# Rotary embedding on one core: the order of three loads on the SP queue

## The chip, the core and the metric

The kernel runs on one core of a Trainium2 chip. The metric is device time in microseconds for one execution, inputs and outputs in device memory (HBM). A core has compute engines that run side by side: TensorE (PE, unused here), VectorE (DVE), ScalarE (ACT) and GpSimd (POOL), and SyncE (SP), which here only issues transfers. Transfers are carried by 16 DMA engines, which all queues share. This kernel uses two queues: SP's, "hardware_dynamic" in the profile, and GpSimd's, "software_dynamic".

## The reference

```python
# x (8, 2048, 16, 64) float32; cos, sin (2048, 32) float32
x_pairs = x.reshape(batch, seq_len, num_heads, head_dim // 2, 2)
x1 = x_pairs[..., 0]
x2 = x_pairs[..., 1]
cos = cos[None, :, None, :].copy()
sin = sin[None, :, None, :].copy()
out1 = x1 * cos - x2 * sin
out2 = x1 * sin + x2 * cos
out = np.stack([out1, out2], axis=-1).reshape(batch, seq_len, num_heads, head_dim)
```

Neighbouring elements of a row form pairs, and each pair is turned by an angle that depends on the position in the sequence and the place in the head. x and the output are 67.1 MB each.

## The kernel before

The work is cut by batch: eight tiles, each a whole batch. Of the 2048 positions a partition holds 16 (`K`), so a batch is a tile of 128 partitions x 16 x 1024 elements: 64 KB a partition in HBM, 32 KB as bfloat16 in SBUF. A load (`load`, line 56) converts from float32 to bfloat16 on the way in, a store (`store`, line 59) converts back on the way out, and both are issued from the GpSimd queue. The pool `xpool` has five tiles (`NX`); batches 5, 6 and 7 take over the tiles of batches 0, 1 and 2, and so their loads wait until those batches are stored.

`rotate` (lines 61 to 80) does the arithmetic in three VectorE instructions: x times a signed sine table into a work tile `qt` (L74), x times a cosine table in place (L75), and the sum of x and `qt` with each pair of `qt` swapped (L80).

The two tables are made once: `sin_sb` and `cos_sb` are loaded from HBM as float32 (256 KB each, 2 KB a partition) and cast by VectorE into `s_tab` (the sine and its negative in turns, L93 and L94) and `c_tab` (each cosine twice, L95).

Batch 0 is split. Its first two positions of each partition (`HEAD`), one megabyte, go by the SP queue as float32 into `head` (line 84), and ScalarE casts them into the tile of batch 0 (L91). The rest of batch 0 comes by the GpSimd queue (`load(0, HEAD)`), followed by batches 1 to 4 whole. So there are two rotations for batch 0, a small one and a large one, and one for every other batch. `head` and `qt` share one buffer (the tag "work", one buffer), so the first rotation also waits until ScalarE has read `head`.

The order is written out by hand (`manual_schedule`): each engine runs its instructions in the order of the program text. On SP these are the megabyte of x (L84), the cosine table (L85), the sine table (L86) and, at the very end, the last store (L119). On GpSimd: five loads; the store of batch 0; a small copy called `mark` (L106), which reads the last element of batch 4 and so holds up all that stands behind it until the fifth load has landed; the store of batch 1; then the load of batch 5, the store of batch 2, the load of batch 6, the store of batch 3, the load of batch 7, and the stores of batches 4 to 7, the last without its final four positions (`TAIL`). Those are cast back by ScalarE (L118) and stored by SP (L119); a one-element copy before them (L117) waits for the store of batch 6.

Of the kernel before, what the change touches and what calls it, by code (L numbers as in the profile page):

```python
# [2 lines left out]

# [4 lines left out]


@with_exitstack  # L10
def kernel(
    ctx: ExitStack,
    tc: tile.TileContext,
    x: bass.AP,
    cos: bass.AP,
    sin: bass.AP,
    out: bass.AP,
):
    nc = tc.nc
    fp32 = mybir.dt.float32  # L20
    bf16 = mybir.dt.bfloat16
    mult = mybir.AluOpType.mult
    add = mybir.AluOpType.add

    B, S, H, D = x.shape
    P = 128
    K = S // P
    KP = 16
    D2 = D // 2
    HD = H * D  # L30
    NX = 5
    HEAD = 2
    TAIL = 4


    x_t = x.rearrange("b (p k) h d -> b p k (h d)", p=P, k=K)
    out_t = out.rearrange("b (p k) h d -> b p k (h d)", p=P, k=K)
    cos_t = cos.rearrange("(p k) c -> p (k c)", p=P, k=K)
    sin_t = sin.rearrange("(p k) c -> p (k c)", p=P, k=K)

    consts = ctx.enter_context(tc.tile_pool(name="consts", bufs=1))
    xpool = ctx.enter_context(tc.tile_pool(name="xpool", bufs=NX))
    stage = ctx.enter_context(tc.tile_pool(name="stage", bufs=1))

    cos_sb = consts.tile([P, K * D2], fp32)
    sin_sb = consts.tile([P, K * D2], fp32)
    c_tab = consts.tile([P, K, D], bf16)
    s_tab = consts.tile([P, K, D], bf16)

    mark = consts.tile([1, 1], bf16)  # L50
    tiles = {}

    def load(b, k0=0):
        if b not in tiles:
            tiles[b] = xpool.tile([P, K, HD], bf16, name="xt")
        nc.gpsimd.dma_start(out=tiles[b][:, k0:], in_=x_t[b, :, k0:])  # L56

    def store(b, k1=K):
        nc.gpsimd.dma_start(out=out_t[b, :, :k1], in_=tiles[b][:, :k1])  # L59

    def rotate(b, k0, k1):
        nk = k1 - k0
        xp = tiles[b][:, k0:k1]
        qt = stage.tile([P, KP, HD], bf16, name="qt", tag="work")

        def rows(a):
            return a.rearrange("p k (h e) -> p k h e", h=H, e=D)

        def tab(a):
            return dataclasses.replace(  # L70
                a, offset=a.offset + k0 * D, ap=[a.ap[0], [D, nk], [0, H], [1, D]]
            )

        nc.vector.tensor_tensor(out=rows(qt[:, :nk]), in0=rows(xp), in1=tab(s_tab), op=mult)  # L74
        nc.vector.tensor_tensor(out=rows(xp), in0=rows(xp), in1=tab(c_tab), op=mult)  # L75
        q_swap = dataclasses.replace(
            qt, offset=qt.offset + 1, ap=[qt.ap[0], [2, nk * HD // 2], [-1, 2]]
        )
        x3 = xp.rearrange("p k (a j) -> p (k a) j", j=2)
        nc.vector.tensor_tensor(out=x3, in0=x3, in1=q_swap, op=add)  # L80

    with tc.manual_schedule():
        head = stage.tile([P, TAIL, HD], fp32, name="st", tag="work")
        nc.sync.dma_start(out=head[:, :HEAD], in_=x_t[0, :, :HEAD])  # L84
        nc.sync.dma_start(out=cos_sb, in_=cos_t)  # L85
        nc.sync.dma_start(out=sin_sb, in_=sin_t)  # L86
        load(0, HEAD)
        for b in range(1, NX):
            load(b)

        nc.scalar.copy(out=tiles[0][:, :HEAD], in_=head[:, :HEAD])  # L91
        s2 = s_tab.rearrange("p k (i j) -> p (k i) j", j=2)
        nc.vector.tensor_copy(out=s2[:, :, 0], in_=sin_sb)  # L93
        nc.vector.tensor_scalar_mul(s2[:, :, 1], sin_sb, -1.0)  # L94
        nc.vector.tensor_copy(  # L95
            out=c_tab.rearrange("p k (i j) -> p (k i) j", j=2),
            in_=cos_sb.to_broadcast([P, K * D2, 2]),
        )
        for b in range(B):
            if b == 0:  # L100
                rotate(b, 0, HEAD)
                rotate(b, HEAD, KP)
            else:
                rotate(b, 0, KP)
            if b == 1:
                nc.gpsimd.tensor_copy(out=mark, in_=tiles[NX - 1][:1, K - 1, :1])  # L106
            if b < B - 1:
                store(b)

            if b >= 1 and b - 1 + NX < B:  # L110
                load(b - 1 + NX)
        store(B - 1, K - TAIL)

        tail = stage.tile([P, TAIL, HD], fp32, name="st", tag="work")
        nc.scalar.copy(out=tiles[B - 2][:1, 0, :1], in_=tiles[B - 1][:1, K - 1, :1])  # L117
        nc.scalar.copy(out=tail, in_=tiles[B - 1][:, K - TAIL :])  # L118
        nc.sync.dma_start(out=out_t[B - 1, :, K - TAIL :], in_=tail)  # L119


# [1 line left out]
_INS = ['x', 'cos', 'sin']  # L123
_OUTS = [((8, 2048, 16, 64), 'float32')]


# [23 lines left out]
```

## Time and profile before

| what | us |
|---|---|
| time, median of 3 runs (317.43 to 317.56) | 317.45 |
| span of the profiled execution | 315.5 |
| VectorE busy | 210.3 |
| ScalarE busy | 6.9 |
| GpSimd busy | 11.7 |
| megabyte of x: from issue to landing | 4.7 |
| cosine table: from issue to landing | 13.4 |
| sine table: from issue to landing | 31.7 |
| first load (rest of batch 0): from issue to landing | 22.3 |

The span runs from the first to the last instruction of the profiled execution, and the time shown for a run is a little longer than it. Lines of the page's first part give each engine's busy time, share of the span and instructions; the row "DMA" gives the mean busy share of the 16 DMA engines in 40 equal slices, in tenths. For a queue the page gives packets, megabytes (as written by the transfer) and the time of its packets as a share of 16 engines' span. In the order of time an entry has its start and its duration in microseconds, the engine, the line of the kernel, the operation, destination and source, and in brackets how long the engine was idle before it and what ended that. An entry of SPq or POOL with DMA_DIRECT2D is the issuing of a transfer, not the transfer. In the table of windows the columns are the window, its length, the busy time of VectorE, ScalarE and GpSimd (with instructions in brackets), the granted TensorE clock, the share of the 16 DMA engines and GB/s. All in all HBM was read for 67.63 MB and written for 67.11 MB.

### The profile page before, as it was taken

Reading aid. Unit: us, or ns where it says so; the run is one execution under the profiler, and the core shown is the slowest. Engines: PE = TensorE matmul, PEld = TensorE weight load, DVE = VectorE, ACT = ScalarE, POOL = GpSimd, SP = SyncE. Lnnn points to the kernel's source line nnn. Section 1 sums busy time; section 2 is a strip of 40 time slices with the busy share of each in tenths; the row PEclk is TensorE's granted clock in tenths of the full one; section 3 lists DMA queues with packets and bytes.
Section 4 is the critical chain, followed back from the end, with each engine's and each line's share of the span. In section 5 each row is a group of like instructions: output and inputs, shape, how many; then the busy total and the mean of one; then the engine's idle time right before and its main releaser. Section 6 shows DMA issues by size and latency. Waiting matters only on the chain.

```text
span 315.5 us, 125 instructions
## 1 busy us (share of the span) xinstructions
DVE 210.3 (67%) x30; ACT 6.9 (2%) x4; POOL 11.7 (4%) x21
## 2 busy tenths in 40 slices
DVE  0000799999999999999999993899509994000000
ACT  4000000000000000000000000000000000000400
POOL 3000000000000301010000100000000000000000
DMA  9899999999999999999999999999999999999997
GB/s 279 184 261 206 199 220 245 199 199 253 212 199 266 399 449 482 399 332 245 220 399 399 399 199 199 399 532 266 199 241 490 399 399 490 440 399 399 432 432 332
DMA packets 2880, 101.71 MB, mean 322 GB/s; under 512 B 320, under 2 KB 320, under 8 KB 576
## 3 DMA queue, kind: packets, MB, share of 16 engines
q0 software_dynamic: 2304, 98.04, 97.1%
q1 hardware_dynamic: 576, 3.67, 3.0%
HBM read 67.63 MB, written 67.11 MB: 427 GB/s over the span
## 4 chain that ended last, share of the span: by engine, by line
another core or an unknown queue 91%; DMA 1%; ACTq 1%; ACT 1%; issue 0%
DMA st<-in_x_dram 1%; ACTq L145 1%; ACT xt L91 1%; ACT xt L117 0%; ACTq L117 0%
## 5 line engine op out<-in xcount | busy, mean ns | idle before, releaser
L74 DVE TENSOR_TENSOR qt<-xt,s_tab 128x16384 bf16<-128x16384 bf16 (+2 forms) x9 | 69.7, 7743 | 19.1 <-DMA xt<-in_x_dram 18.8
L75 DVE TENSOR_TENSOR xt<-xt,c_tab 128x16384 bf16<-128x16384 bf16 (+2 forms) x9 | 69.7, 7743 | 0.4
L80 DVE TENSOR_TENSOR xt<-xt,qt 128x16384 bf16<-128x16384 bf16 (+2 forms) x9 | 69.7, 7744 | 0.3
L93 DVE CAST s_tab<-sin_sb 128x512 bf16<-128x512 f32 x1 | 0.5, 453 | 33.4 <-DMA sin_sb<-in_sin_dram 33.4
L59 POOL DMA_DIRECT2D out_dram<-xt x8 | 4.3, 534 | 139.9 <-DVE xt L80 139.9
L56 POOL DMA_DIRECT2D xt<-in_x_dram x8 | 4.4, 560 | 72.8 <-DMA out_dram<-xt 72.0
L117 ACT COPY xt<-xt 1x1 bf16<-1x1 bf16 x1 | 0.2, 192 | 288.0 <-DMA out_dram<-xt 288.0
L106 POOL COPY mark<-xt 1x1 bf16<-1x1 bf16 x1 | 2.9, 2929 | 39.6 <-DMA xt<-in_x_dram 39.6
L118 ACT CAST st<-xt 128x4096 f32<-128x4096 bf16 x1 | 3.6, 3598 | 0.0
L91 ACT CAST xt<-st 128x2048 bf16<-128x2048 f32 x1 | 1.9, 1897 | 3.4 <-DMA st<-in_x_dram 3.4
L91 ACT ACT_TABLE_LOAD x1 | 1.3, 1283 | 0.7 <-PEq L134 0.7
L95 DVE CAST c_tab<-cos_sb 128x1024 bf16<-128x1024 f32 x1 | 0.7, 683 | 0.0
L94 DVE TENSOR_SCALAR s_tab<-sin_sb 128x512 bf16<-128x512 f32 x1 | 0.4, 444 | 0.0
L134 POOL MEMSET const-float32-0.0<- 128x1 f32 x1 | 0.1, 100 | 0.2 <-issue 0.2
L134 POOL MEMSET const-bfloat16-1.0<- 128x1 bf16 x1 | 0.1, 102 | 0.0
L134 POOL MEMSET const-float32-1.0<- 128x1 f32 x1 | 0.1, 100 | 0.0
L134 POOL MEMSET const-uint8-127<- 128x1 uint8 x1 | 0.1, 100 | 0.0
## 6 DMA issues: line engine op xcount, KB each, us to landing
xt<-in_x_dram POOLq DMA_DIRECT2D x7, 4096.0 KB, 57.6
out_dram<-xt POOLq DMA_DIRECT2D x1, 6144.0 KB, 47.8
xt<-in_x_dram POOLq DMA_DIRECT2D x1, 3584.0 KB, 22.3
out_dram<-st SPq DMA_DIRECT2D x1, 2048.0 KB, 15.5
st<-in_x_dram SPq DMA_DIRECT2D x1, 1024.0 KB, 4.7
cos_sb<-in_cos_dram SPq DMA_DIRECT2D x1, 256.0 KB, 13.4
sin_sb<-in_sin_dram SPq DMA_DIRECT2D x1, 256.0 KB, 31.7
out_dram<-xt POOLq DMA_DIRECT2D x7, 70.1
```

The lines of the kernel that those rows point to most:

```text
L56: nc.gpsimd.dma_start(out=tiles[b][:, k0:], in_=x_t[b, :, k0:])
L59: nc.gpsimd.dma_start(out=out_t[b, :, :k1], in_=tiles[b][:, :k1])
L74: nc.vector.tensor_tensor(out=rows(qt[:, :nk]), in0=rows(xp), in1=tab(s_tab), op=mult)
L75: nc.vector.tensor_tensor(out=rows(xp), in0=rows(xp), in1=tab(c_tab), op=mult)
L80: nc.vector.tensor_tensor(out=x3, in0=x3, in1=q_swap, op=add)
L91: nc.scalar.copy(out=tiles[0][:, :HEAD], in_=head[:, :HEAD])
L93: nc.vector.tensor_copy(out=s2[:, :, 0], in_=sin_sb)
L94: nc.vector.tensor_scalar_mul(s2[:, :, 1], sin_sb, -1.0)
L95: nc.vector.tensor_copy(out=c_tab.rearrange("p k (i j) -> p (k i) j", j=2), in_=cos_sb.to_broadcast([P, K * D2, 2]),)
L106: nc.gpsimd.tensor_copy(out=mark, in_=tiles[NX - 1][:1, K - 1, :1])
L118: nc.scalar.copy(out=tail, in_=tiles[B - 1][:, K - TAIL :])
L145: with _tile.TileContext(nc) as tc:
```

## The change

The three issues at the head of the SP queue change places: cosine table, sine table, megabyte of x. The same three transfers are issued from the same queue, and the other queues and engines keep their instructions and their order.

```diff
     with tc.manual_schedule():
         head = stage.tile([P, TAIL, HD], fp32, name="st", tag="work")
-        nc.sync.dma_start(out=head[:, :HEAD], in_=x_t[0, :, :HEAD])
         nc.sync.dma_start(out=cos_sb, in_=cos_t)
         nc.sync.dma_start(out=sin_sb, in_=sin_t)
+        nc.sync.dma_start(out=head[:, :HEAD], in_=x_t[0, :, :HEAD])
         load(0, HEAD)
         for b in range(1, NX):
             load(b)
```

So lines 84, 85 and 86 are the cosine table, the sine table and the megabyte of x in the changed kernel; all other line numbers stay.

## The prediction

> **What bounds the kernel now.** I read the page first, for what is busy from end to end.
>
> ```profile
> span 315.5 us, 125 instructions
> DVE 210.3 (67%) x30; ACT 6.9 (2%) x4; POOL 11.7 (4%) x21
> DMA  9899999999999999999999999999999999999997
> q0 software_dynamic: 2304, 98.04, 97.1%
> q1 hardware_dynamic: 576, 3.67, 3.0%
> ```
>
> No compute engine is near full, but the packets of the two queues add up to 100.1% of sixteen engines' span. So the transfers are the bound, and nearly all are on q0, the GpSimd queue; q1 is SP's. Behind the 4% of GpSimd lies only the issuing. The counts also give the shape: 20 transfers (four on SP, sixteen on GpSimd) share 2880 packets, 144 each, nine on each of sixteen engines: eight rows of data (128 partitions over 16 engines) and one small closing packet (the page counts 320 under 512 B, which is 20 x 16).
>
> Second, the order of time, for what the moved transfers feed.
>
> ```profile
> 0.74 0.36 SPq L84 DMA_DIRECT2D st<-in_x_dram  x1
> 1.16 0.42 SPq L85 DMA_DIRECT2D cos_sb<-in_cos_dram  x1
> 1.24 2.80 POOL L56 DMA_DIRECT2D xt<-in_x_dram  x5 [0.80 <-PEq L145]
> 1.63 0.42 SPq L86 DMA_DIRECT2D sin_sb<-in_sin_dram  x1
> 5.45 1.90 ACT L91 CAST xt<-st 128x2048 bf16<-128x2048 f32 x1 [3.43 <-DMA st<-in_x_dram]
> 33.38 0.45 DVE L93 CAST s_tab<-sin_sb 128x512 bf16<-128x512 f32 x1 [33.38 <-DMA sin_sb<-in_sin_dram]
> 38.43 7.62 DVE L74 TENSOR_TENSOR qt<-xt,s_tab 128x14336 bf16<-128x14336 bf16 x1
> 61.93 0.54 POOL L59 DMA_DIRECT2D out_dram<-xt  x1 [57.89 <-DVE xt L80]
> 102.11 2.93 POOL L106 COPY mark<-xt 1x1 bf16<-1x1 bf16 x1 [39.64 <-DMA xt<-in_x_dram]
> 121.68 0.53 POOL L56 DMA_DIRECT2D xt<-in_x_dram  x1 [16.17 <-DMA out_dram<-xt]
> ```
>
> VectorE sits idle for 33.38 us until the sine table is there, although the first piece of x was there at 5.43. But the first store, issued at 61.93, lands only at 121.68, 19.6 us after the fifth load landed (102.11). By the rate of full transfers (8.39 MB in 19.3 us, below) 19.6 us is one store's own length: it had been waiting in the queue behind the loads. VectorE's lateness is hidden there.
>
> Third, short windows of the start, for what the transfer engines carry. The columns I use are the last two, DMA share and GB/s; a packet is counted whole in the window in which it begins, so that 6.00 to 7.00 shows nothing while long packets run.
>
> ```profile
> 1.00:2.00 1.00, 0.00 (x0) 1.00 (x1) 0.76 (x2) 1.00 0.39 66
> 2.00:3.00 1.00, 0.00 (x0) 0.02 (x1) 1.00 (x3) 1.00 0.74 254
> 3.00:4.00 1.00, 0.00 (x0) 0.00 (x0) 1.00 (x2) 1.00 1.00 418
> 4.00:5.00 1.00, 0.00 (x0) 0.00 (x0) 0.04 (x1) 1.00 0.93 375
> 5.00:6.00 1.00, 0.00 (x0) 0.55 (x1) 0.00 (x0) 1.00 2.50 602
> 6.00:7.00 1.00, 0.00 (x0) 1.00 (x1) 0.00 (x0) 1.00 0.00 0
> ```
>
> The loads begin with a burst a little after 5.0: one row of the first load on each of 16 engines is 3584 KiB / 8 = 459 KB, and the window has 602. The rest, 143 KB, and the windows before it are SP's: 66 + 254 + 418 + 375 + 143 = 1256 KB of the 1573 KB that its three transfers hold.
>
> **The change, part by part.** No instruction is added or removed; three issues on SP swap places, and the megabyte is passed by two transfers of 256 KB.
>
> *The tables.* They start at 0.74 and 1.16. The windows reach 524 KB (both tables) at 3.5 us; the megabyte, which had begun whole at about 4.8, landed at 5.43, so I add 0.6: landed at about 4.1 instead of 14.56 (1.16 + 13.4) and 33.3 (1.63 + 31.7). The three table casts (33.38 to 34.66, 1.28 us) run at 4.1 to 5.4.
>
> *The megabyte.* By the start of the loads 1256 KB have gone as before, of them now 1256 - 524 = 732 KB of its 1049: 5.6 rows of 8 on an engine. What is left takes turns with load rows. The trace shows the price of a turn: the sine table's nine packets landed 18.8 us after the cosine table, 2.09 us each. Two to four rows and the closing packet, three to five turns, end at 11.7 to 15.9; I take 14. The outer bounds are 6.2 (317 KB at the 418 GB/s of the full window, no turns) and 33.4 (27 packets of SP's, as before, if their number alone decides). None is later than the sine table now.
>
> *VectorE.* The ACT copy (1.90 us) ends at about 16, the small rotation (34.66 to 38.43, 3.8 us) at 20, and the next waits for the first load, which lands at 1.24 + 22.3 = 23.5 as before. So its big run starts at 23.5 instead of 38.43: 14.9 us gained on VectorE. What is late next is the loads: VectorE keeps its waits for the loads of batches 6 and 7, and gets a new one for batch 5.
>
> *The store queue, where the gain stops.* The first store is issued at 47 instead of 61.93, behind the same five loads, which end at 102. The next GpSimd step, the mark, waits for the fifth load at 102.11, not for VectorE; the sixth load waits for the first store to land. From there all issues have the same releasers: I cost the gain at nothing, and the cover is the loads' 102 us, 40 us longer than VectorE needed before.
>
> *The mark's phase.* The mark ended at 105.04 just as a vector multiply did (96.31 + 8.69 = 105.00). With VectorE shifted the multiply then running is that of batch 3 and ends at 107.6 (23.5 + 23.0 + 2 x 26.2 = 98.9, + 8.7). The second store is issued 2.6 us later, 13 us before the first has landed: no cost. If the queue did run dry here, up to 5 us.
>
> *The transfers themselves.* The bytes are the same. All of SP's packets cost 3.0% of 315.5 = 9.5 us on an engine; at 418 GB/s they would cost 8.8. So a better order can save at most 0.7 us. A worse one: the first window's 66 KB at a share of 0.39 are 169 GB/s, at which the tables would take 3.1 us instead of 1.25, +1.85 us. The nearest row is the one with full engines (418), as cold-start latency is paid once in either order: 0, perhaps -0.1.
>
> *The casts beside the first issues.* New is that VectorE works at 4.1 to 5.4 while the first loads get under way (GpSimd's five issues end at 4.04, the rows begin at 5.1). Lower bound 0. Upper: the rows start 1.1 us (5.1 - 4.04) after the casts, at 6.5 to 7.0, while SP's rows cover until 5.4 + 317/418 = 6.2: 0.3 to 0.8 us of idle engines. GpSimd's other issues beside busy VectorE took 0.53 to 0.54 us, no longer than beside an idle one, so I take 0.
>
> Here the Trainium skill speaks against the change ("SBUF — State Buffer", "SBUF: two separate sides"): transfers from the GpSimd queue need descriptors that GpSimd writes through a port which VectorE holds during some of its operations, and they starve until it is done. The mark agrees with a held port; no run here shows it for descriptors. By the rule the sum would be 0.3 to 0.8 us more, by the rows nothing.
>
> **Sum.** 315.5 + 0 - 0.1 = 315.4 us of span; the median, 317.45, lies 1.95 above the profiled span, and that part is not touched: 317.4 us.
>
> **Rivals.** *A: the earlier VectorE shortens the run.* For it: 33.4 us of idle time at the head. If VectorE were on the path, 317.45 - 14.9 = 302.6. Against it: its waits for batches 6 and 7.
>
> ```profile
> 198.72 8.69 DVE L74 TENSOR_TENSOR qt<-xt,s_tab 128x16384 bf16<-128x16384 bf16 x1 [6.40 <-DMA xt<-in_x_dram]
> 237.32 8.69 DVE L74 TENSOR_TENSOR qt<-xt,s_tab 128x16384 bf16<-128x16384 bf16 x1 [12.45 <-DMA xt<-in_x_dram]
> ```
>
> Whatever it gains it hands back at 198.72. (38.6 us between them is a load and a store, 19.3 us each.)
>
> *B, slower: the casts hold up the first loads' start.* Place: 4 to 7 us. It decides if the first load rows begin over 0.6 us after SP's rows have run out, so after 6.8. With casts 0.5 us later than I reckon (tables at 4.6) and the full 1.1 us behind them the idle is 0.8, with a second 0.5 us 1.3: 318.1 to 318.8, say 318.4. The mark's phase is a smaller way to the same side.
>
> *C, faster: a stall in the loads goes away.* The last windows of the first loads carry the usual bytes at a higher share.
>
> ```profile
> 50.00:60.00 10.00, 9.97 (x2) 0.00 (x0) 0.00 (x0) 1.00 0.97 210
> 90.00:100.00 10.00, 9.97 (x2) 0.00 (x0) 0.00 (x0) 1.00 1.06 210
> ```
>
> 0.09 x 10 us = 0.9 us whose cause the trace doesn't show. If it comes from where VectorE stands then, it may be gone: 316.5. Against: the same vector operations run at 50 to 60 without it.
>
> *D: the swap does not bring the megabyte in sooner than the sine table came.* By count of turns (27) it lands at about 33. VectorE is then where it was: 317.45, part of the forecast.
>
> **How the numbers follow.** A measurement of this kernel tells about 0.2% (0.63 us) from no change. Forecast with D: 0.76, 316.9 to 318.0. B with the mark: 0.13, nearly all above 318.08. C: 0.09, and A 0.02, both below 316.8. The range takes in C's 316.5 nearly and the lower half of B's span: 316.6 to 318.4. Faster 0.11, same 0.76, slower 0.13.
>
> **What would show it.** The sine cast should start at about 4, the ACT copy at about 14, the first big multiply at 23.5 and the first store's issue at 47; the mark should still start at 102.1, the sixth load's issue at 121.7, and batch 6's multiply at 198.7 with a wait for its load. If the mark starts later than 102.3, the start was lost to B; if it starts before 101.5, C. I am wrong outright if the sixth load's issue moves by more than a microsecond, since then something other than the queue's order sets it.

## The result: slower by 0.4%, and the profile after

The changed kernel takes 319.18 us (median of 7 runs, 317.9 to 319.75) against 317.56 (7 runs, 317.33 to 317.77). The ratio of the runs is put at 1.0039, 95% interval 1.0028 to 1.0050: slower, by 0.9 to 1.6 us (the medians alone give 1.0051, 1.62 us). The runs also lie much further apart than before: 1.85 us from the lowest to the highest, against 0.44.

The page of the changed kernel, in the lines that answer to those shown of before:

```profile
span 317.6 us, 125 instructions
DVE 210.4 (66%) x30; ACT 6.9 (2%) x4; POOL 13.7 (4%) x21
DMA  7999999999999999999999999999999999999995
q0 software_dynamic: 2304, 98.04, 96.6%
q1 hardware_dynamic: 576, 3.67, 2.9%
```

The packets are the same and take the same time; the row of the DMA engines has lost something in the first slice (7 for 9) and in the last (5 for 7). The order of time, changed kernel:

```profile
0.74 0.38 SPq L84 DMA_DIRECT2D cos_sb<-in_cos_dram  x1
1.17 0.42 SPq L85 DMA_DIRECT2D sin_sb<-in_sin_dram  x1
1.64 0.42 SPq L86 DMA_DIRECT2D st<-in_x_dram  x1
4.16 0.45 DVE L93 CAST s_tab<-sin_sb 128x512 bf16<-128x512 f32 x1 [4.16 <-DMA sin_sb<-in_sin_dram]
28.07 1.90 ACT L91 CAST xt<-st 128x2048 bf16<-128x2048 f32 x1 [26.05 <-DMA st<-in_x_dram]
33.78 7.63 DVE L74 TENSOR_TENSOR qt<-xt,s_tab 128x14336 bf16<-128x14336 bf16 x1
57.29 0.54 POOL L59 DMA_DIRECT2D out_dram<-xt  x1 [53.25 <-DVE xt L80]
104.25 4.87 POOL L106 COPY mark<-xt 1x1 bf16<-1x1 bf16 x1 [46.42 <-DMA xt<-in_x_dram]
123.83 0.54 POOL L56 DMA_DIRECT2D xt<-in_x_dram  x1 [14.23 <-DMA out_dram<-xt]
```

The tables are there at 4.16 and VectorE's large multiply starts 4.65 us sooner than before. Yet the fifth load lands 2.14 us later (104.25 for 102.11), and all that follows is shifted by the same amount (the sixth load's issue by 2.15). So the time went in the first loads, on the transfers' side. The windows of the start, changed kernel (share of the DMA engines and GB/s last; a packet counts where it begins):

```profile
2.00:3.00 1.00, 0.00 (x0) 0.02 (x1) 1.00 (x3) 1.00 0.84 291
3.00:4.00 1.00, 0.00 (x0) 0.00 (x0) 1.00 (x2) 1.00 2.45 578
4.00:5.00 1.00, 0.84 (x3) 0.00 (x0) 0.04 (x1) 1.00 0.39 57
5.00:6.00 1.00, 0.52 (x1) 0.00 (x0) 0.00 (x0) 1.00 0.68 160
```

Count it through. Up to 4.0 us 29 + 291 + 578 = 898 KB have begun (29 in the window 1 to 2). Both tables are 524 KB; the other 374 KB are 13 load rows of 28.7 KB (459 KB / 16). So on 13 of the 16 DMA engines the loads begin before 4.0, not after 5.0. Half-microsecond windows place the other three:

```profile
3.50:4.00 0.50, 0.00 (x0) 0.00 (x0) 0.50 (x2) 1.00 3.27 668
4.00:4.50 0.50, 0.34 (x1) 0.00 (x0) 0.04 (x1) 1.00 0.00 0
4.50:5.00 0.50, 0.50 (x3) 0.00 (x0) 0.00 (x0) 1.00 0.78 115
5.00:5.50 0.50, 0.50 (x1) 0.00 (x0) 0.00 (x0) 1.00 0.39 57
```

115 GB/s over half a microsecond are two rows, 57 one. Three DMA engines began their first load row one to two microseconds after the others (the trace has them at 4.90, 4.95 and 5.07, the last of the others at 3.82), and in between no packet of any queue began. These rows are slow as well: a share of 0.78 over half a microsecond is 6.2 us of packet time for two rows, 3.1 us each, and 0.39 is 3.1 us for the third, where a turn later in the trace takes 2.09. So about half of the 2.14 us may be the gap and half the slow rows behind it; that is an estimate from these rows, and no run parts the two. An engine has its own eight rows of each transfer, so the others cannot take over what it is late. The windows of the end agree; first the kernel before, then the changed one:

```profile
313.00:314.00 1.00, 0.00 (x0) 0.00 (x0) 0.00 (x0) 1.00 0.65 279
314.00:315.00 1.00, 0.00 (x0) 0.00 (x0) 0.00 (x0) 1.00 0.01 0
```

```profile
313.00:314.00 1.00, 0.00 (x0) 0.00 (x0) 0.00 (x0) 1.00 0.84 360
314.00:315.00 1.00, 0.00 (x0) 0.00 (x0) 0.00 (x0) 1.00 0.20 82
315.00:316.00 1.00, 0.00 (x0) 0.00 (x0) 0.00 (x0) 1.00 0.19 82
```

Before, no data packet begins after 314. In the changed kernel 82 KB, five 16 KB packets of the last store, begin in each of the next two microseconds. A share of 0.19 to 0.20 is three engines of sixteen, as many as were late at the start: they set the end.

### The profile page after: what moved, and what is told of

It is laid out like the page before. It is cut to its first block, busy times and chain, and to the rows that moved or that the text cites. A ratio compares the mean times of both kernels' runs of the same rounds, so it can differ in the third digit from the quotient of the medians.

```text
span 317.6 us, 125 instructions
## 1 busy us (share of the span) xinstructions
DVE 210.4 (66%) x30; ACT 6.9 (2%) x4; POOL 13.7 (4%) x21
## 4 chain that ended last, share of the span: by engine, by line
another core or an unknown queue 84%; DMA 8%; ACTq 1%; ACT 1%; SPq 0%; issue 0%
DMA st<-in_x_dram 8%; ACTq L145 1%; ACT xt L91 1%; SPq L85 0%; SPq L84 0%; ACT xt L117 0%; ACTq L117 0%
## 5 line engine op out<-in xcount | busy, mean ns | idle before, releaser
L106 POOL COPY mark<-xt 1x1 bf16<-1x1 bf16 x1 | 4.9, 4867 | 46.4 <-DMA xt<-in_x_dram 46.4
## 6 DMA issues: line engine op xcount, KB each, us to landing
st<-in_x_dram SPq DMA_DIRECT2D x1, 1024.0 KB, 26.4
```

## The experiments

Each ratio is to the kernel before, measured beside it. Two theories stood at first: **held port** (the early VectorE casts keep GpSimd from getting the loads under way, rival B of the prediction) and **dry queue** (SP's small packets are through at 3.5 us, and some DMA engines then have nothing to do, casts or not).

### Casts held back

The changed order; a one-element copy makes VectorE wait for the megabyte before it casts the tables.

```diff
+        held = consts.tile([1, 1], bf16)
+        nc.vector.tensor_copy(out=held, in_=tiles[0][:1, 0, :1])
         s2 = s_tab.rearrange("p k (i j) -> p (k i) j", j=2)
```

> The changed order of the three loads, with the table casts held back until ScalarE has cast the megabyte (one VectorE copy of one element, some 0.1 us, not on the path). Theory 'held port': the casts at 4.2 to 5.5 keep GpSimd from starting the loads on some DMA engines; without them there the loss goes, 317.4 to 317.7 us, as close from run to run as before. Theory 'dry queue': the small table packets are done by 3.5 and some DMA engines then have nothing until about 5, casts or not; 318.2 to 319.6 us, with runs as far apart as in the changed kernel, and the window 4 to 5 us has a DMA share far below 1 with the next windows not making it up.

Measured: 319.12 us, ratio 1.0043 (1.0019 to 1.0067), runs from 317.18 to 319.81. VectorE does nothing until 29 us, and the windows of this run show the late rows all the same:

```profile
3.50:4.00 0.50, 0.00 (x0) 0.00 (x0) 0.50 (x2) 1.00 3.43 742
4.00:4.50 0.50, 0.00 (x0) 0.00 (x0) 0.04 (x1) 1.00 0.79 115
4.50:5.00 0.50, 0.00 (x0) 0.00 (x0) 0.00 (x0) 1.00 0.36 57
5.00:5.50 0.50, 0.00 (x0) 0.00 (x0) 0.00 (x0) 1.00 0.00 0
```

The casts are not the cause. Two of its seven runs were as quick as the kernel before (317.18 and 317.23), the others at 319.0 to 319.8. So the same program has the loss in some runs and not in others.

### Casts that nothing needs, in the order of before

```diff
+        dsrc = consts.tile([P, K * D2], fp32)
+        ddst = consts.tile([P, K * D2, 2], bf16)
+        nc.vector.memset(dsrc, 0.0)
+        for _ in range(20):
+            nc.vector.tensor_copy(out=ddst[:, :, 0], in_=dsrc)
         s2 = s_tab.rearrange("p k (i j) -> p (k i) j", j=2)
```

> The order of before, with a memset and 20 VectorE casts of the form of the sine cast (0.34 us apart) on a tile that nothing reads, from 0.8 to about 8 us. Theory 'held port': the first load rows come later than 5.1, up to about 8, and the time grows by 1 to 3 us. Theory 'dry queue': nothing changes, 317.3 to 317.7 us, first load rows in the window 5 to 6.

Measured: 318.02 us, ratio 1.0018 (1.0010 to 1.0027). The casts ran from 1.4 to 11.2 us, GpSimd's five issues took 2.90 us instead of 2.80, and the load rows still began in the window 5 to 6. Neither theory had this: VectorE at work through the whole start costs some 0.6 us, but it neither delays the loads by microseconds nor spreads the runs as the change does. With 1.3 us of casts in the changed kernel and the first experiment's 319.12 without them, no part of the loss could be put down to it.

### The megabyte between the tables, and the megabyte on ScalarE's queue

Two runs that give the DMA engines something larger. Against the changed kernel, the first:

```diff
         nc.sync.dma_start(out=cos_sb, in_=cos_t)
-        nc.sync.dma_start(out=sin_sb, in_=sin_t)
         nc.sync.dma_start(out=head[:, :HEAD], in_=x_t[0, :, :HEAD])
+        nc.sync.dma_start(out=sin_sb, in_=sin_t)
```

> Cosine table, megabyte, sine table: the same casts' form, but 8 KB packets stand among the first sixteen packets of an engine on SP's queue. Theory 'dry queue': the DMA engines are covered until the loads begin near 5, 317.2 to 317.8 us with close runs; the sine table lands at 20 to 25 us or so and VectorE's start moves there, which costs nothing. Theory 'held port': also 317.2 to 317.8, since the casts wait for the late sine table, so this run tells only whether the place of the small packets alone matters: if it is over 318.2, both fall.

Measured: 317.40 us, ratio 0.9997 (0.9989 to 1.0006). The second:

```diff
-        nc.sync.dma_start(out=head[:, :HEAD], in_=x_t[0, :, :HEAD])
+        nc.scalar.dma_start(out=head[:, :HEAD], in_=x_t[0, :, :HEAD])
```

> Tables on SP's queue as in the changed kernel, the megabyte issued from ScalarE's queue at 0.7 us, so that DMA engines have a third queue with work in it from about 2 us. Theory 'dry queue': no DMA engine runs out before the loads begin, 317.2 to 317.8 us with close runs. Theory 'held port': the tables land early (4 to 5 us), the casts run at 4 to 6 as in the changed kernel, and the loss stays, 318.2 to 319.6 us, unless the megabyte's rows cover the wait, in which case the first load rows begin after 5.5 and the window share stays near 1.

Measured: 317.53 us, ratio 1.0002 (0.9993 to 1.0010). In both the engines are covered until the loads begin, which is again in the window 5 to 6; the window 4 to 5 of the two runs, in this order:

```profile
4.00:5.00 1.00, 0.00 (x0) 0.00 (x0) 0.04 (x1) 1.00 0.98 410
```

```profile
4.00:5.00 1.00, 0.00 (x0) 0.00 (x0) 0.04 (x1) 1.00 1.07 424
```

Both fit the dry queue. They say nothing on the held port, as the sine table came late in both (28.5 and 24.3 us); in the second it had been expected at 4 to 5.

### The loads 8 us and 2 us later

Why has an engine nothing to do at 4 us, with the megabyte issued at 1.64? Either its packets are not there yet (**late megabyte**), or the engine has turned to the loads and waits for them (**held engine**). With n = 16 and n = 4, on the changed order:

```diff
+        pause = consts.tile([P, K * D2], fp32)
+        for _ in range(n):
+            nc.gpsimd.memset(pause, 0.0)
         load(0, HEAD)
```

> The changed order, with 16 GpSimd memsets of a 128x512 tile that nothing reads ahead of the first load, so that SP's queue has the DMA engines to itself for some 8 us more. Two readings of the dry queue stand against each other. 'Late megabyte': its packets are not there when the tables are through at 3.5, loads or not; then the windows show a hole near 4 to 5 us before the megabyte's packets. 'Held engine': the packets are there, but an engine that has done some 16 packets of SP's turns to the loads and stays with them until their first row, even while it waits; then, with no loads in the queue, the megabyte's packets follow the tables without a hole, the windows 2 to 6 us all have a share near 1, and the ScalarE cast starts at 6 to 7. The time itself grows by the wait in either case, to 321 to 326 us.

Measured: 324.02 us (two runs), ratio 1.0212 (1.0193 to 1.0231). The loads are issued at 10.81, so SP's queue has the engines to itself:

```profile
3.50:4.00 0.50, 0.00 (x0) 0.00 (x0) 0.44 (x2) 1.00 0.55 168
4.00:4.50 0.50, 0.40 (x2) 0.00 (x0) 0.44 (x2) 1.00 0.73 213
4.50:5.00 0.50, 0.50 (x2) 0.00 (x0) 0.50 (x1) 1.00 0.52 164
```

Once the tables are through, the engines carry 164 to 213 GB/s, about half of the 324 to 426 that the kernel before moves in the same windows. ScalarE's cast starts at 8.91, not at 6 to 7. The megabyte is late on a part of the engines, with no load in any queue: late megabyte, though not a hole on all of them.

> The same with 4 memsets, so that the loads are issued some 2 us later than in the changed kernel, when SP's queue still has the megabyte. 'Held engine': more of the megabyte goes ahead of the loads, the DMA engines turn to rows that are ready sooner after, and most of the loss goes, 317.2 to 318.2 us. 'Late megabyte': the hole at 4 to 5 us stays and the loads do not fill it, 319 to 321 us.

Measured: 318.81 us, ratio 1.0055 (1.0043 to 1.0068), between the two expectations; it does not tell them apart.

### The megabyte in quarters

The order of before, in transfers as small as the tables.

```diff
-        nc.sync.dma_start(out=head[:, :HEAD], in_=x_t[0, :, :HEAD])
+        for k in range(HEAD):
+            for j in range(0, HD, HD // 2):
+                nc.sync.dma_start(
+                    out=head[:, k, j : j + HD // 2], in_=x_t[0, :, k, j : j + HD // 2]
+                )
```

> The order of before, with the megabyte cut into four transfers of 256 KB (2 KB a partition), so that its bytes still go first but the first 18 packets of an engine on SP's queue are as small as the tables'. If it is the number of SP's packets that decides when the engines turn to the loads, the first load rows begin at 3.4 to 3.8 as in the changed kernel and it is as slow: 318.2 to 319.6 us with runs far apart. If it is when the loads are ready (5.1 in the kernel before), nothing changes: 317.3 to 317.8, first rows in the window 5 to 6.

Measured: 336.87 us, ratio 1.0618 (1.0604 to 1.0633). The start is that of the changed kernel although x goes first:

```profile
3.00:4.00 1.00, 0.00 (x0) 0.00 (x0) 1.00 (x2) 1.00 2.61 633
4.00:5.00 1.00, 0.00 (x0) 0.00 (x0) 0.03 (x1) 1.00 0.18 29
```

Up to 4.0 us 29 + 264 + 633 = 926 KB: two of SP's small transfers (524 KB) and 14 load rows. So it is small packets at the head of SP's queue that let the loads in early, not the tables as such. The 19 us are another matter and were not expected: six transfers of SP's are 54 packets on an engine; the first two transfers, 18 packets, go before the loads, the other 36 take turns with load rows, and the sine table lands at 85.27. Then VectorE is no longer hidden (the next run has the same).

### The loads alone

SP's three transfers, in the order of before, wait for the first load. In the program text the five loads now stand ahead of the copy that is added:

```diff
+        nc.scalar.copy(out=head[:1, 0, :1], in_=tiles[0][:1, HEAD, :1])
         nc.sync.dma_start(out=head[:, :HEAD], in_=x_t[0, :, :HEAD])
```

> SP's three transfers in the order of before, but issued only when the first load has landed (a ScalarE copy of one element into the megabyte's buffer, ahead of its load, makes them wait), so the loads start with nothing beside them. It measures the loads' own start: the time from the issue at 1.24 to the first rows on the first and on the last of the 16 DMA engines. If the loads' first rows come by themselves at 3.4 on some engines and at 5 or later on others, the changed kernel's late engines are the loads' own unevenness, uncovered; the last windows then show a few engines late too, and the time is 319.5 to 321.5 us. If all first rows come within 0.5 us, the unevenness comes from SP's packets beside them, and the time is the earlier idle alone, 318.5 to 320 us.

Measured: 337.50 us, ratio 1.0654 (1.0627 to 1.0680). The start is what it was made for:

```profile
2.00:2.50 0.50, 0.00 (x0) 0.02 (x1) 0.50 (x2) 1.00 0.00 0
2.50:3.00 0.50, 0.00 (x0) 0.00 (x0) 0.50 (x2) 1.00 4.82 745
3.00:3.50 0.50, 0.00 (x0) 0.00 (x0) 0.50 (x2) 1.00 0.94 172
```

745 GB/s over half a microsecond are 13 rows, 172 are three: by themselves the loads begin on all sixteen engines between 2.5 and 3.5 us, the first at most 1.8 us behind the issue at 1.24. Their start was never the 5.1 us that the kernel before shows; there they stood behind SP's packets. The time is another matter again: as in the quarters VectorE starts late, at 85.54, the first store is issued at 114.09, and the transfer engines stand empty for it:

```profile
101.00:114.00 13.00, 12.93 (x3) 0.00 (x0) 0.00 (x0) 1.00 0.00 0
```

### The other loads later, in both orders

One more suspicion was that the first rows are slow because GpSimd is still issuing the other four loads (**issuing beside**), against a cold start that has no such cause. The changed order with n = 10, the order of before with n = 5:

```diff
         load(0, HEAD)
+        pause = consts.tile([P, K * D2], fp32)
+        for _ in range(n):
+            nc.gpsimd.memset(pause, 0.0)
         for b in range(1, NX):
```

> The changed order, with 10 GpSimd memsets (some 6 us) between the issue of the first load and that of the other four, so that GpSimd issues nothing while the first load's first rows run. Theory 'issuing beside': the loads' first rows are slow (2.2 to 3.5 us instead of 2.1) because GpSimd still writes the other loads; here they are not, and the part of the loss that comes from it goes; what stays are the DMA engines that find neither a load row nor a packet of the megabyte after 3.5: 317.8 to 318.8 us. Theory 'cold start': a queue's first row is slow whenever the DMA engines come to it early; nothing changes, 318.2 to 319.7 us.

Measured: 318.33 us (317.12 to 319.99), ratio 1.0037 (1.0019 to 1.0055). There is still a loss, but 318.33 lies in both forecasts.

> The order of before, with 5 memsets between the first load and the other four, so that these are issued at about 5 to 7.5, just when the first load's first rows begin. 'Issuing beside': the first rows are now slow and the DMA engines uneven, 317.9 to 319 us though the order of the loads is that of before. 'Cold start': 317.2 to 317.8 us as before.

Measured: 317.30 us, ratio 0.9997 (0.9988 to 1.0006). Here GpSimd issues from 4.72 to 6.84, just as the first rows run, and nothing is lost: issuing beside is not enough to make the loss. That it adds to it in the changed order is not excluded, as five of the twelve runs there are under 317.8 and none of the seven of the changed kernel. The run of the first that was profiled happened to be its quickest, 317.12 us, and shows the same program without the loss:

```profile
3.00:4.00 1.00, 0.00 (x0) 0.00 (x0) 0.88 (x3) 1.00 2.78 684
4.00:5.00 1.00, 0.88 (x2) 0.00 (x0) 0.94 (x2) 1.00 0.00 0
```

4 + 295 + 684 = 983 KB up to 4.0 us are the tables and all 16 load rows. When every engine finds a load row as the tables end, nothing is lost; when a few don't, up to 2.6 us are (319.99 against 317.36).

### Third place, or packets ahead

> Cosine table in two transfers of 64 partitions, then the megabyte, then the sine table: the megabyte is the third transfer on SP's queue, as in the changed kernel, but only some ten small packets of an engine stand ahead of it instead of eighteen. If the third transfer is late because of the number of packets ahead, it is on time here and the time is 317.2 to 317.8 us, first load rows near 5. If it is late because it is the third transfer, the windows 3 to 5 us show a hole or load rows from 3 us, and the time is 318.2 to 320 us.

```diff
-        nc.sync.dma_start(out=cos_sb, in_=cos_t)
-        nc.sync.dma_start(out=sin_sb, in_=sin_t)
+        nc.sync.dma_start(out=cos_sb[: P // 2], in_=cos_t[: P // 2])
+        nc.sync.dma_start(out=cos_sb[P // 2 :], in_=cos_t[P // 2 :])
         nc.sync.dma_start(out=head[:, :HEAD], in_=x_t[0, :, :HEAD])
+        nc.sync.dma_start(out=sin_sb, in_=sin_t)
```

Measured: 317.77 us, ratio 1.0012 (1.0003 to 1.0020), runs from 317.53 to 318.31.

```profile
2.00:3.00 1.00, 0.00 (x0) 0.02 (x1) 1.00 (x3) 1.00 2.23 418
3.00:4.00 1.00, 0.00 (x0) 0.00 (x0) 1.00 (x2) 1.00 0.97 172
```

590 KB are all 16 load rows (459 KB) and one half of the cosine table (131 KB): here SP's queue was dry behind its first transfer already, so the run does not tell a third place from a number of packets. It does show that an early start of the loads is cheap, some 0.4 us, when all engines turn to them together.

### The sine table on ScalarE's queue

```diff
-        nc.sync.dma_start(out=sin_sb, in_=sin_t)
+        nc.scalar.dma_start(out=sin_sb, in_=sin_t)
```

> Cosine table and then the megabyte on SP's queue, the sine table on ScalarE's, both tables issued at 0.7 us: the same sixteen small data packets of an engine go first as in the changed kernel, but the megabyte is issued second on its queue, at 1.2 instead of 1.6 us, and behind nine packets instead of eighteen. If the loss comes from the megabyte's packets not being there when the tables are through, the DMA engines are covered here: share near 1 in the windows 2 to 5 us, first load rows near 5, 317.2 to 317.7 us with close runs. If sixteen small packets at the start cost the time whatever stands behind them, first load rows near 3.5 and 318.2 to 319.7 us.

Measured: 317.15 us (316.95 to 317.35), ratio 0.9993 (0.9984 to 1.0002).

```profile
3.50:4.00 0.50, 0.00 (x0) 0.00 (x0) 0.50 (x2) 1.00 1.21 475
4.00:4.50 0.50, 0.00 (x0) 0.00 (x0) 0.04 (x1) 1.00 1.15 479
4.50:5.00 0.50, 0.19 (x1) 0.00 (x0) 0.00 (x0) 1.00 0.98 410
5.00:5.50 0.50, 0.50 (x3) 0.00 (x0) 0.00 (x0) 1.00 0.97 410
```

No gap, though the tables go first. The loss is gone with one transfer moved to another queue, so the tables' going first is not by itself the cause. With it gone where the megabyte follows in time (here and on ScalarE's queue), and the megabyte late behind the two tables even without loads (n = 16), the cause is that its packets are not there when the tables end, on engines that have no load row yet. This version also has what the change was able to give VectorE: casts at 4.81, the first rotation at 15.39, the first store issued at 47.67. It gains nothing that can be told from zero by it.

## Why the prediction was wrong

- **The bound** was right. VectorE's start does not matter so long as the first store is issued before the fifth load lands: it moved forward by 4.65 us here and by 14 in the last experiment without a gain, and back by 52 us in the loads-alone run for 20 us. The margin read from the trace (61.93 against 102.11) was real. The mark's phase cost nothing either, as forecast: it ended at 109.12 instead of 105.04, well before the first store had landed (123.83).
- **The step that failed** is the megabyte's: "By the start of the loads 1256 KB have gone as before". It took the 5.1 us at which the loads begin in the kernel before for the loads' own start, and let SP's queue feed the engines until then whatever stood in it. Alone, the loads begin at 2.5 to 3.5 us. What held them until 5.1 was SP's queue: 1256 KB are the megabyte and 207 KB of the cosine table, nine packets and some six more on an engine, and these went ahead of load rows that were ready. With the megabyte among the first packets that lasts until 5.1; the two tables, 18 packets, are through at 3.5. Instead of 732 KB of the megabyte, none had gone when the loads began. By the prediction's own sign this is wrong outright: the sixth load's issue moved by 2.15 us.
- **The megabyte's landing** followed from that: all of its nine packets took turns, and it landed at 28, near the outer bound of 33.4 and not at the 14 taken. The first large multiply came at 33.78 instead of 23.5, the first store at 57.29 instead of 47. This cost nothing.
- **The cost of the swap on the transfers**, taken as 0 to -0.1 with +1.85 as the bound, is the term that was mis-sized: about +1.2 us by the ratio, +1.6 by the medians, +2.1 in the profiled run. The bound was worked from a cold start of small packets; the loss is three engines with nothing to do behind them and the slow load rows that they then run (3.1 us). That the bound of +1.85 is of the same size is chance.
- **Rival B** had the place (4 to 7 us), the sign and nearly the size (318.4), and its sign in the trace came true (the mark after 102.3). Its mechanism, the casts, was wrong: without them the time is 319.12.
- **Rival C**: the share of 1.06 for the same bytes at 90 to 100 us is still there (below). **D** was nearest for the megabyte's landing, but it was priced at nothing.

On the Trainium skill. The rule that spoke against the change ("SBUF — State Buffer", "SBUF: two separate sides") did not cause the loss here: with the casts held back the time is 319.12 us, and a lasting run of casts beside the start cost 0.6 us. Another rule bears on the step that failed: by "DMA: Bandwidth & Descriptors", "Queues, rings and completion order", a DMA engine goes round the queues that it has work for and takes a whole packet, typically about 9 to 17 descriptors, from one before it turns to the next. In the kernel before, the windows up to 5.0 hold SP's packets alone (66 + 254 + 418 + 375 KB, with no load row), though the loads alone begin from 2.5 us, and an engine runs some 15 packets of SP's before its first load row. A packet of the profile is one row of a transfer here; if it is what the page calls a descriptor, which no run shows, these 15 agree with the page. Later in the trace SP's packets go one to a turn, at 2.09 us a turn, and don't.

What stays open: why a transfer behind others on SP's queue is late on some engines, why some engines find no load row at 3.5 us when the loads alone were under way on all sixteen by then, and why these engines' first load rows are slow.

## What to carry to other kernels

Where transfers bound the kernel and each engine has a fixed share of them, as here, the engine that starts last can set the end: three engines, one to two microseconds late, moved it by 2.1 us. Look at the first microseconds in half-microsecond windows and count packets, not the mean share. When a queue's first transfer moves, ask what it was holding back and for how long it feeds the engines; the time at which the next queue begins in the old trace may belong to the first queue. Where small transfers have to go early, try one of them on another queue: with the sine table on ScalarE's the ratio to the kernel before was 0.9993 (317.15 us), with both tables ahead of the megabyte on SP's 1.0039 (319.18 us).

## What the runs showed that was not expected

Near 100 us the load rows of most profiled runs stall for up to 1.0 us: the window 95 to 100 has a share of 1.15 before, 1.13 after, 1.17 with the megabyte in the middle, all at the usual 210 GB/s. In the quarters and the loads-alone run, where no store stands in the queue behind the fifth load, it is 0.97. So in these profiles it goes with the first store waiting there; the later changes from load to store were not looked into, and no run removed it on its own, so its cause is not shown.

In these runs SP's queue, where it had to take turns, paid by the packet and not by the byte: nine packets of the sine table took 18.8 us in the kernel before, and the megabyte took 4.7 us in front, 26.4 us behind the tables, and cut into quarters landed with the tables behind it at 45 and 85 us.
